# Half-width products for the dilated groups, and a head's values placed in front of the next head's scores

## The chip, the cores and the metric

The kernel runs on one core of one Trainium2 chip. The metric is the device time of one execution in microseconds (us); the time before is the median of three runs. TensorE (PE in the profile) multiplies matrices: the stationary operand is loaded by a weight load (PEld), then the other operand is streamed through it, and the result lands in PSUM. PSUM has eight banks here, each of 128 partitions by 512 words. VectorE (DVE), ScalarE (ACT) and GpSimd (POOL) work beside TensorE, and SyncE (SP) starts the loads of the weights from memory.

## What is computed

Two residual layers over 256 tokens of width 1024. The first mixes tokens with a gated short convolution, the second with dilated attention, and each has an MLP and a gated embedding behind it. The change is in the attention, which has eight heads of width 128. Each head is computed three times, in groups with three patterns of (window, dilation), and the three results are weighted by a softmax over their log-sums, which is the same as one softmax over all scores of the three groups together:

```python
DILATED_PATTERNS = ((128, 1), (512, 4), (2048, 16))
...
s = jnp.einsum('nbqhd,nbkhd->nbhqk', qb, kk) * (dh ** -0.5)
band = (rel >= 0) & (rel <= n_back)
...
o_g, lse_g = dilated_window_attention(q[:, :, g], k[:, :, g], v[:, :, g], window, dilation)
weights = jax.nn.softmax(jnp.stack(lses, axis=0), axis=0)
o = jnp.sum(weights[..., None] * jnp.stack(outs, axis=0), axis=0)
```

In group 1 a token attends only to tokens of its own residue modulo 4, in group 2 only to its own residue modulo 16.

## The kernel before

**Number formats.** Most products are made of operands split into a high and a low part (`hi`, `lo`, format fp32r): `lo*hi`, `hi*lo` and `hi*hi` are added up in one bank. Every loaded weight slab is split by ACT (L357, `whi`) and DVE (L296, `wlo`). The products of groups 1 and 2 in the attention are plain fp32 instead: L684 for the scores, L724 for the values.

**Layout.** From the second layer on, tokens are ordered by `residue_order` (L41): 64 tokens of one residue modulo 4 follow each other. There are two blocks `b` of 128 tokens, so that each block holds two whole residues, in its first and its second 64 rows. Group 1 and group 2 therefore need only the products of a block with itself, and of these only the two squares of 64 by 64 on the diagonal; the other two squares are computed too and are masked out.

**A head's steps.** `qk_out` rotates queries and keys (from the second head on, on POOL: L647 to L656), `qk_split` splits group 0. `v_out` (L662) scales the values out of the two banks `acc_v`: group 0 split into `v0`, groups 1 and 2 into `v12`. `scores` (L674) makes, for each block, three fp32r products of 256 columns for group 0 (L681) and one fp32 product of 128 by 128 for each of the groups 1 and 2 (L684), all in one bank of 512 columns; then mask and maximum (L687), exponential (L691) and division (L693) give the weights `sm`. `turn` (L695) transposes them: the half that belongs to groups 1 and 2 on DVE in squares of 32 (L701, L704), group 0 on TensorE (L708). `values` (L711) adds up the head's output in one bank: six fp32r products for group 0 (L718), then four fp32 products of 128 by 128 for groups 1 and 2 (L724); L735 and L736 split the result into `y`.

**The order.** `make_plan` (L139) writes down one list of blocks of weights (`w`, `n`, `t`: two or three products each, all issued at L393) and steps (`do`). TensorE follows it. In the loop over heads `h` (L199 to L206) the blocks of head `h` alternate with the steps of head `h-1`: `scores` stands behind the blocks of group 0, `turn` behind those of group 2, and `values` between the values' blocks 5 and 6. Head 1 is later by one place, and `values` of head 0 then stands in head 2. The last head's steps are laid between the blocks of the output projection `w_o`: three rounds of `w_o`, `scores`, two rounds, `turn`, one round, `values`, two rounds. A scheduler orders each engine's instructions by this program order, and puts in the waits.

**Buffers.** All banks come from one pool of eight (L262). Weights are split five slabs ahead of their use (`LOOK`, L34).

Of the kernel before, what the change touches and what calls it, by code (L numbers as in the profile page):

```python
# [9 lines left out]
F32 = mybir.dt.float32  # L10
# [5 lines left out]
P = 128  # L16
S = 256
# [237 lines left out]
def tile_trunk(ctx: ExitStack, tc: tile.TileContext, plan, slabs, ap, out):  # L255
# [11 lines left out]
    def act(name, dtype=F32):  # L267
        return apool.tile([P, 2, S], dtype, tag="act", name=name)
# [23 lines left out]
    def flat(t):  # L292
        return t.rearrange("p i s -> p (i s)")
# [285 lines left out]

    def masks_load():  # L580
        for b in (0, 1):
            mask[b] = apool.tile([P, 512], F32, tag="act", name=f"mask{b}")
            nc.sync.dma_start(mask[b], ap["mask"][:, b, :])

    def conv(c):
# [75 lines left out]

    def v_out(head):  # L662

        v0, v12 = act(f"v0_{head}", F32R), act(f"v12_{head}")
        for b in (0, 1):
            p, r = flat(close(("v", b, head))), rstd[3][:, b : b + 1]
            hi, lo = v0[:, b, :P], v0[:, b, P:]
            nc.scalar.activation(hi, p[:, :P], AF.Copy, scale=r)
            nc.vector.scalar_tensor_tensor(lo, p[:, :P], r, f32(hi), ALU.mult, ALU.subtract)
            nc.scalar.activation(v12[:, b, :], p[:, P : GROUPS * P], AF.Copy, scale=r)  # L670
        cur["v", head] = v0, v12


    def scores(head):  # L674
        weights = cur["pr", head] = pair(f"sm{head}", dtype=F32)[2]
        for b in (0, 1):
            own = slice(b * P, (b + 1) * P)
            ps = psum.tile([P, 512], F32, tag="ps", name=f"sc{head}_{b}")
            hi, lo, _ = state["qk"][head]
            for n, (q, k) in enumerate(((hi, hi), (hi, lo), (lo, hi))):  # L680
                nc.tensor.matmul(ps[:, :S], q[:, 0, own], k[:, 1, :], start=n == 0, stop=n == 2)  # L681
            for g in (1, 2):
                t = cur["qk", head, g]
                nc.tensor.matmul(ps[:, (g + 1) * P : (g + 2) * P], t[:, 0, own], t[:, 1, own], start=True, stop=True)  # L684
            sm = flat(weights[:, b])
            stats = [spool.tile([P, 1], F32, tag=f"st{n}_{b}", name=f"st{n}_{head}_{b}") for n in range(3)]
            nc.vector.tensor_tensor_reduce(  # L687
                out=sm, in0=ps, in1=mask[b], op0=ALU.add, op1=ALU.max, scale=SCALE, scalar=NEG, accum_out=stats[0]
            )
            nc.vector.tensor_scalar(stats[1], stats[0], -1.0, None, ALU.mult)  # L690
            nc.scalar.activation(sm, sm, AF.Exp, bias=stats[1], accum_out=stats[2])  # L691
            nc.vector.reciprocal(stats[2], stats[2])
            nc.scalar.activation(sm, sm, AF.Copy, scale=stats[2])  # L693

    def turn(head):  # L695

        sm = cur.pop(("pr", head))
        t = cur["pT12", head] = act(f"pT12_{head}")  # L700
        nc.vector.transpose(t, sm[:, :, 1, :])  # L701
        for q in range(4):
            rows, cols = (slice(n * 32, (n + 1) * 32) for n in (q, q ^ 1))
            nc.vector.transpose(t[cols, :, rows], sm[rows, :, 1, cols])  # L704
        ps = bank(f"tp{head}")
        for b in (0, 1):
            for n in (0, 1):
                nc.tensor.transpose(ps[:, n, b * P : (b + 1) * P], sm[:, b, 0, n * P : (n + 1) * P], ident)  # L708
        split_into("pT", head, ps)

    def values(head):  # L711
# [7 lines left out]
                    ps[:, 0, :], a, b[:, kb, :], start=kb == 0 and n == 0, stop=False, skip_group_check=True  # L719
                )  # L720
        t = cur.pop(("pT12", head))
        for b in (0, 1):
            for g in (0, 1):
                nc.tensor.matmul(  # L724
                    ps[:, 0, b * P : (b + 1) * P],
                    v12[:, b, g * P : (g + 1) * P],
                    t[:, b, g * P : (g + 1) * P],
                    start=False,
                    stop=g == 1,
                    skip_group_check=True,  # L730
                )
        if head % 2 == 0:
# [120 lines left out]
def masks():  # L853

    import numpy as np

    t = np.argsort([residue_order(t) for t in range(S)])
    m = np.full((P, 2, 512), NEG, np.float32)
    for b in range(2):
        q = t[b * P : (b + 1) * P, None]  # L860
        for keys, to, window, step in (
            (t, slice(0, S), 128, 1),
            (t[b * P : (b + 1) * P], slice(S, S + P), 512, 4),
            (t[b * P : (b + 1) * P], slice(S + P, S + 2 * P), 2048, 16),
        ):
            d = q - keys[None]
            m[:, b, to][(d >= 0) & (d <= window) & (d % step == 0)] = 0.0
    return m


# [56 lines left out]
```

## Time and profile before

| quantity | value |
|---|---|
| median of three runs | 777.29 us (777.19 to 777.32) |
| the profiled execution, its own time | 777.36 us |
| its span in the profile | 775.5 us |
| attention with its output projection | about 306 to 560 us of the span |
| one head in the steady state, from `scores` to `scores` | 28.63 us (395.49 to 424.12) |

How to read it: the span is what the hardware profiler saw, and 1.9 us of the device time lie around it. A row of a group of instructions gives the source line, the engine, the operation, output and inputs by name, shapes and the count; then busy time and the mean duration of one; then idle time of that engine ahead of them and what ended it. A row of a timeline gives the start in us, the length from the first start to the last end, and the same names; neighbours on one engine are merged with their count. TensorE's products are pipelined: one lasts longer than the distance to the next one's start, so costs on TensorE are read from distances of starts and not from durations. An fp32 product is two instructions on TensorE, each with a weight load of its own, so L684 and L724 have 64 instructions each for 32 products.

### The profile page before, as it was taken

How to read it: one execution, taken by the hardware profiler on the slowest of the kernel's cores; microseconds unless marked ns; L12 is line 12 of the kernel's file. 1: busy time of each engine (PE TensorE's matmuls, PEld its weight loads, DVE VectorE, ACT ScalarE, POOL GpSimd, SP SyncE). 2: the span in 40 equal slices, each digit the busy share in tenths (PEclk: the TensorE clock that was granted, in tenths of full speed). 3: DMA queues.
4: the chain of work that ended last, by engine and by line, in shares of the span. 5: the costliest groups of instructions: out<-in, count | busy, mean ns of one | idle time of the engine just before them, and what ended most of it. 6: DMA issues, size and time to landing. Idle time of an engine off the chain costs nothing.

```text
span 775.5 us, 12403 instructions
## 1 busy us (share of the span) xinstructions
PE 766.9 (99%) x4780; PEld 696.3 (90%) x4780; DVE 595.5 (77%) x863; ACT 439.4 (57%) x677; POOL 167.1 (22%) x110
## 2 busy tenths in 40 slices
PE   9999999999999999999999999999999999999996
PEld 8998998888888899989999989989988888888885
DVE  6898779898566668789789889887798887555664
ACT  7655565565444446557655655655665555444454
POOL 0000000000000000078867867865000000000002
PEclk9999999999999999999999999999999999999999
DMA  8965655655565554654546445456465655555521
GB/s 313 301 192 187 187 184 180 195 187 191 190 188 190 191 190 138 210 182 157 170 150 183 158 152 188 150 161 208 135 211 181 190 188 188 188 188 191 190 93 54
DMA packets 42538, 140.95 MB, mean 182 GB/s; under 512 B 4848, under 2 KB 6128, under 8 KB 42480
## 3 DMA queue, kind: packets, MB, share of 16 engines
q1 hardware_dynamic: 41904, 139.52, 55.9%
q8 instruction: 37, 0.61, 0.3%
q10 hardware_dynamic: 576, 0.66, 0.3%
q14 instruction: 21, 0.17, 0.1%
HBM read 139.10 MB, written 1.05 MB: 181 GB/s over the span
## 4 chain that ended last, share of the span: by engine, by line
PE 97%; issue 1%; DMA 1%; DVE 0%; POOL 0%; SPq 0%; POOLq 0%; DVEq 0%; ACT 0%
PE acc_u L393 23%; PE acc_d L393 23%; PE acc_qk L393 17%; PE acc_v L393 9%; PE acc_o L393 6%; PE acc_g L393 5%; PE acc_B L393 3%; PE acc_C L393 3%; PE acc_X L393 3%; PE o L724 1%; PE sc L684 1%; PE acc_p L393 1%; PE o L718 1%; PE sc L681 1%; DMA pt<-in_pT 1%
## 5 line engine op out<-in xcount | busy, mean ns | idle before, releaser
L296 DVE TENSOR_TENSOR wlo<-raw,whi 128x1024 fp32r<-128x1024 f32 (+2 forms) x277 | 353.2, 1280 | 125.6 <-ACT whi L357 122.7
L357 ACT ACTIVATE whi<-raw 128x1024 fp32r<-128x1024 f32 (+2 forms) x277 | 278.2, 1007 | 214.3 <-PE acc_d L393 77.1
L393 PE MATMUL acc_d<-u,whi 128*128 128x512 f32 x512 | 160.8, 395 | 0.0
L393 PE MATMUL acc_u<-x,whi 128*128 128x512 f32 x512 | 160.8, 395 | 0.0
L393 PE MATMUL acc_qk<-x,whi 128*128 128x512 f32 (+1 forms) x432 | 134.5, 368 | 0.0
L393 PEld LDWEIGHTS acc_d<-u,wlo 128*128 128x128 f32 x512 | 96.2, 188 | 22.7
L393 PEld LDWEIGHTS acc_u<-x,wlo 128*128 128x128 f32 x512 | 96.2, 188 | 22.5
L463 POOL TENSOR_TENSOR n<-v,power 128x2 f32<-128x2 f32 (+1 forms) x6 | 3.9, 650 | 517.1 <-DVE v L488 512.6
L393 PE MATMUL acc_qk<-x,wlo 128*128 128x256 f32 x384 | 108.0, 281 | 0.0
L393 PE MATMUL acc_u<-x,wlo 128*128 128x256 f32 x512 | 101.2, 278 | 0.0
L393 PE MATMUL acc_d<-u,wlo 128*128 128x256 f32 x512 | 100.9, 278 | 0.0
L393 PEld LDWEIGHTS acc_qk<-x,whi 128*128 128x128 f32 x432 | 78.0, 189 | 13.6
L650 POOL TENSOR_TENSOR rot<-qk,sinr 16x512 f32<-16x512 f32 x44 | 78.5, 1785 | 3.0
L393 PEld LDWEIGHTS acc_d<-u,whi 128*128 128x128 f32 x512 | 78.0, 189 | 0.0
L393 PEld LDWEIGHTS acc_u<-x,whi 128*128 128x128 f32 x512 | 78.0, 189 | 0.0
L393 PEld LDWEIGHTS acc_qk<-x,wlo 128*128 128x128 f32 x384 | 72.6, 189 | 0.0
L393 PE MATMUL acc_v<-whi,x 128*128 128x384 f32 x256 | 69.0, 340 | 0.0
L647 POOL TENSOR_TENSOR qk<-qk,cosr 128x512 f32<-128x512 f32 x22 | 37.4, 1698 | 51.4 <-DVE qk L413 41.0
L393 PEld LDWEIGHTS acc_v<-whi,x 128*128 128x128 f32 x256 | 46.6, 188 | 0.0
L393 PE MATMUL acc_o<-y,whi 128*128 128x256 f32 x256 | 46.3, 283 | 0.0
L393 PE MATMUL acc_v<-wlo,x 128*128 128x384 f32 x128 | 42.9, 335 | 0.0
L656 POOL TENSOR_TENSOR qk<-qk,rot 48x512 f32<-48x512 f32 x22 | 42.3, 1924 | 1.7
(176 smaller groups left out, 1036.2 us busy)
## 6 DMA issues: line engine op xcount, KB each, us to landing
raw<-in_w SPq DMA_DIRECT2D x230, 512.0 KB, 4.0
raw<-in_w SPq DMA_DIRECT2D x32, 384.0 KB, 3.1
raw<-in_w SPq DMA_DIRECT2D x10, 256.0 KB, 5.0
h<-in_xT SPq DMA_DIRECT2D x4, 256.0 KB, 5.0
mask<-in_mask SPq DMA_DIRECT2D x2, 256.0 KB, 4.3
gain<-in_gain SPq DMA_DIRECT2D x2, 256.0 KB, 4.3
out<-htg SPq DMA_DIRECT2D x2, 256.0 KB, 2.1
raw<-in_w ACTq DMA_DIRECT2D x2, 128.0 KB, 3.6
```

The source lines that it names most:

```text
L296: nc.vector.tensor_tensor(out, a, f32(b), ALU.subtract)
L357: nc.scalar.activation(hi[:, :width], t[:, :width], AF.Copy)
L393: nc.tensor.matmul(to, a, b, start=n == 0 and name not in opened, stop=n == len(products) - 1 and left[name, half if kind == "n" else 0] == 0,
L463: nc.gpsimd.tensor_tensor(y, v, power[:, : v.shape[1]], ALU.pow)
L647: engine.tensor_tensor(t, p, both(cosr), ALU.mult)
L650: engine.tensor_tensor(r[dst : dst + 16], p[src : src + 16], sinr[src : src + 16].unsqueeze(1).to_broadcast([16, 2, S]), ALU.mult,)
L656: engine.tensor_tensor(t[:48], t[:48], r[:48], ALU.add)
L681: nc.tensor.matmul(ps[:, :S], q[:, 0, own], k[:, 1, :], start=n == 0, stop=n == 2)
L684: nc.tensor.matmul(ps[:, (g + 1) * P : (g + 2) * P], t[:, 0, own], t[:, 1, own], start=True, stop=True)
L718: nc.tensor.matmul(ps[:, 0, :], a, b[:, kb, :], start=kb == 0 and n == 0, stop=False, skip_group_check=True)
L724: nc.tensor.matmul(ps[:, 0, b * P : (b + 1) * P], v12[:, b, g * P : (g + 1) * P], t[:, b, g * P : (g + 1) * P], start=False, stop=g == 1, ...
```

## The change

The products of groups 1 and 2 shrink to the squares of 64 by 64 that are needed, and their operands are stored accordingly: in a block's 64 rows of one residue, the scores of group 1 stand at the residue's own place and those of group 2 at the other's, so that both groups together take 128 columns in place of 256. `v_out` stores the values of groups 1 and 2 stacked in the same way, in one piece for each block, residue and group. The values' products are cut into halves of 64 output rows, whose squares write to the first or the second 64 partitions of the bank; so do those of the scores. The step `values` of a head no longer has a place of its own in the plan (except for the last head): `scores` of the next head calls it first, and the half-width products of both follow each other.

```diff
     for h in range(1, HEADS):
-        late, steps = h == 1, [[("do", what, h - 1)] for what in ("scores", "turn", "values")]
-        plan += qk(h, 0, range(NK)) + ([("do", "values", 0)] if h == 2 else []) + sums(h, 0)
-        plan += [("do", "qk_split", 0)] if late else steps[0]
-        plan += qk(h, 1, range(NK)) + sums(h, 1) + qk(h, 2, range(NK)) + steps[late ^ 1] + sums(h, 2)
-        plan += v(h, range(3)) + [("do", "qk_split", h)] + v(h, range(3, 6)) + steps[2 - late]
+        late, scores, turn = h == 1, [("do", "scores", h - 1)], [("do", "turn", h - 1)]
+        plan += qk(h, 0, range(NK)) + sums(h, 0) + ([("do", "qk_split", 0)] if late else scores)
+        plan += qk(h, 1, range(NK)) + sums(h, 1) + qk(h, 2, range(NK)) + (scores if late else turn) + sums(h, 2)
+        plan += v(h, range(3)) + [("do", "qk_split", h)] + v(h, range(3, 6)) + (turn if late else [])
...
-    plan += [x for k in (0, 1, 2) for j in range(NP) for x in mix("w_o", j, (k,))]
+    plan += [x for k in (0, 1) for j in range(NP) for x in mix("w_o", j, (k,))]
     plan.append(("do", "scores", last))
-    plan += [x for k in (3, 4) for j in range(NP) for x in mix("w_o", j, (k,))]
+    plan += [x for k in (2, 3, 4) for j in range(NP) for x in mix("w_o", j, (k,))]
...
 def v_out(head):
-            nc.scalar.activation(v12[:, b, :], p[:, P : GROUPS * P], AF.Copy, scale=r)
+            for r in (0, 1):
+                own, other = (slice(n * 64, (n + 1) * 64) for n in (r, 1 - r))
+                for g, to in ((1, own), (2, other)):
+                    nc.scalar.activation(
+                        v12[to, b, r * P : (r + 1) * P], p[own, g * P : (g + 1) * P], AF.Copy, scale=scale[own]
+                    )
...
 def scores(head):
+        if head:
+            values(head - 1)
         weights = cur["pr", head] = pair(f"sm{head}", dtype=F32)[2]
+        ps = [psum.tile([P, 512], F32, tag="ps", name=f"sc{head}_{b}") for b in (0, 1)]
+        for b in (0, 1):
+            for g in (1, 2):
+                t = cur["qk", head, g]
+                for r in (0, 1):
+                    of, at = slice(b * P + r * 64, b * P + (r + 1) * 64), S + (g - 1 ^ r) * 64
+                    nc.tensor.matmul(
+                        ps[b][r * 64 : (r + 1) * 64, at : at + 64], t[:, 0, of], t[:, 1, of], start=True, stop=True
+                    )
         for b in (0, 1):
...
-            for g in (1, 2):
-                t = cur["qk", head, g]
-                nc.tensor.matmul(ps[:, (g + 1) * P : (g + 2) * P], t[:, 0, own], t[:, 1, own], start=True, stop=True)
-            sm = flat(weights[:, b])
+            sm, p = flat(weights[:, b])[:, : S + P], ps[b][:, : S + P]
...
 def turn(head):
-        nc.vector.transpose(t, sm[:, :, 1, :])
-        for q in range(4):
-            rows, cols = (slice(n * 32, (n + 1) * 32) for n in (q, q ^ 1))
+        nc.vector.transpose(t[:, :, :P], sm[:, :, 1, :P])
+        for q, k in ((0, 1), (1, 0), (0, 2), (1, 3), (2, 0), (3, 1), (2, 3), (3, 2)):
+            rows, cols = (slice(n * 32, (n + 1) * 32) for n in (q, k))
             nc.vector.transpose(t[cols, :, rows], sm[rows, :, 1, cols])
...
 def values(head):
-        for b in (0, 1):
-            for g in (0, 1):
+        for n in range(4):
+            q, b, r = slice(n * 64, (n + 1) * 64), n // 2, n % 2
+            for m in (0, 1):
+                to = slice(m * 64, (m + 1) * 64)
                 nc.tensor.matmul(
-                    ps[:, 0, b * P : (b + 1) * P],
-                    v12[:, b, g * P : (g + 1) * P],
-                    t[:, b, g * P : (g + 1) * P],
+                    ps[to, 0, q],
+                    v12[:, b, r * P + m * 64 : r * P + (m + 1) * 64],
+                    t[:, b, r * 64 : (r + 1) * 64],
```

The masks shrink from 512 to 384 columns, with group 1 and 2 at the stacked places. With them the mask step (L687), the exponential (L691) and the division (L693) work on 384 columns in place of 512.

More of the change, by code (lines that the diff above doesn't have):

```diff
@@ L581, in masks_load @@
         for b in (0, 1):
-            mask[b] = apool.tile([P, 512], F32, tag="act", name=f"mask{b}")
+            mask[b] = apool.tile([P, S + P], F32, tag="act", name=f"mask{b}")
             nc.sync.dma_start(mask[b], ap["mask"][:, b, :])
@@ L665, in v_out @@
         for b in (0, 1):
-            p, r = flat(close(("v", b, head))), rstd[3][:, b : b + 1]
+            p, scale = flat(close(("v", b, head))), rstd[3][:, b : b + 1]
             hi, lo = v0[:, b, :P], v0[:, b, P:]
-            nc.scalar.activation(hi, p[:, :P], AF.Copy, scale=r)
-            nc.vector.scalar_tensor_tensor(lo, p[:, :P], r, f32(hi), ALU.mult, ALU.subtract)
-            nc.scalar.activation(v12[:, b, :], p[:, P : GROUPS * P], AF.Copy, scale=r)
+            nc.scalar.activation(hi, p[:, :P], AF.Copy, scale=scale)
@@ L671, in v_out @@
+            nc.vector.scalar_tensor_tensor(lo, p[:, :P], scale, f32(hi), ALU.mult, ALU.subtract)
+            for r in (0, 1):
[4 more added lines that the diff above has]
+                    )
         cur["v", head] = v0, v12
     def scores(head):
+        if head:
+            values(head - 1)
@@ L676, in scores @@
         for b in (0, 1):
             own = slice(b * P, (b + 1) * P)
-            ps = psum.tile([P, 512], F32, tag="ps", name=f"sc{head}_{b}")
             hi, lo, _ = state["qk"][head]
             for n, (q, k) in enumerate(((hi, hi), (hi, lo), (lo, hi))):
-                nc.tensor.matmul(ps[:, :S], q[:, 0, own], k[:, 1, :], start=n == 0, stop=n == 2)
-            for g in (1, 2):
-                t = cur["qk", head, g]
-                nc.tensor.matmul(ps[:, (g + 1) * P : (g + 2) * P], t[:, 0, own], t[:, 1, own], start=True, stop=True)
@@ L685, in scores @@
-            sm = flat(weights[:, b])
+                nc.tensor.matmul(ps[b][:, :S], q[:, 0, own], k[:, 1, :], start=n == 0, stop=n == 2)
+            sm, p = flat(weights[:, b])[:, : S + P], ps[b][:, : S + P]
             stats = [spool.tile([P, 1], F32, tag=f"st{n}_{b}", name=f"st{n}_{head}_{b}") for n in range(3)]
             nc.vector.tensor_tensor_reduce(
-                out=sm, in0=ps, in1=mask[b], op0=ALU.add, op1=ALU.max, scale=SCALE, scalar=NEG, accum_out=stats[0]
+                out=sm, in0=p, in1=mask[b], op0=ALU.add, op1=ALU.max, scale=SCALE, scalar=NEG, accum_out=stats[0]
@@ L721, in values @@
         t = cur.pop(("pT12", head))
[L722 to L723 removed]
+        for n in range(4):
+            q, b, r = slice(n * 64, (n + 1) * 64), n // 2, n % 2
+            for m in (0, 1):
+                to = slice(m * 64, (m + 1) * 64)
                 nc.tensor.matmul(
[L725 to L727 removed]
+                    ps[to, 0, q],
+                    v12[:, b, r * P + m * 64 : r * P + (m + 1) * 64],
+                    t[:, b, r * 64 : (r + 1) * 64],
                     start=False,
[L729 removed]
+                    stop=n == 3,
                     skip_group_check=True,
@@ L857, in masks @@
     t = np.argsort([residue_order(t) for t in range(S)])
-    m = np.full((P, 2, 512), NEG, np.float32)
+    m = np.full((P, 2, S + P), NEG, np.float32)
     for b in range(2):
         q = t[b * P : (b + 1) * P, None]
[L861 to L867, printed above, removed]
+        for r, rows in enumerate((slice(0, 64), slice(64, P))):
+            own = t[b * P : (b + 1) * P][rows]
+            for keys, at, window, step in (
+                (t, 0, 128, 1),
+                (own, S + r * 64, 512, 4),
+                (own, S + (1 - r) * 64, 2048, 16),
+            ):
+                d = q[rows] - keys[None]
+                m[rows, b, at : at + len(keys)][(d >= 0) & (d <= window) & (d % step == 0)] = 0.0
     return m
```

## The prediction

> **What bounds the kernel now.** I read the page first: the engines' shares, the granted clock, the chain that ended last.
>
> ```profile
> span 775.5 us, 12403 instructions
> PE 766.9 (99%) x4780; PEld 696.3 (90%) x4780; DVE 595.5 (77%) x863; ACT 439.4 (57%) x677; POOL 167.1 (22%) x110
> PEclk9999999999999999999999999999999999999999
> PE 97%; issue 1%; DMA 1%; DVE 0%; POOL 0%; SPq 0%; POOLq 0%; DVEq 0%; ACT 0%
> ```
>
> TensorE is busy for 99% of the span at full granted clock, and the chain is TensorE for 97%. A busy TensorE may still wait inside, so next comes the view of waits, asked for TensorE alone:
>
> ```profile
> PE warm L523 <- DVE power L519: 1.0, 1, 1.0
> PE acc_p L393 <- ACT whi L357: 0.2, 1, 0.2
> ```
>
> Two waits, both in the first microseconds (L523 is the warm-up); from there TensorE waits for nobody. So only TensorE time counts for this change, as long as the others keep their lead. Are they ahead?
>
> ```profile
> L357 ACT ACTIVATE whi<-raw 128x1024 fp32r<-128x1024 f32 (+2 forms) x277 | 278.2, 1007 | 214.3 <-PE acc_d L393 77.1
> 388.60:417.25 28.65, 28.65 (x178) 26.60 (x177) 24.50 (x34) 17.02 (x29) 20.89 (x13) 1.00 0.53 166
> ```
>
> ACT's splitting of weights waits for TensorE to free buffers (214.3 us of idle time ahead of it), so the supply of weights runs ahead. The second row is a window of one head's length, with busy time of PE, PEld, DVE, ACT, POOL: 28.65 us of TensorE beside 24.50 of DVE and 17.02 of ACT.
>
> **What the products cost now.** One head's `values`, then one head's `scores`, on TensorE's timeline, and the groups of the fp32 products:
>
> ```profile
> 385.90 0.33 PE L393 MATMUL acc_v<-wlo,x 128*128 128x384 f32 x1
> 386.07 0.33 PE L393 MATMUL acc_v<-whi,x 128*128 128x384 f32 x1
> 386.25 0.87 PE L718 MATMUL o<-pT,v 128*128 128x256 f32 x6
> 386.96 1.05 PE L724 MATMUL o<-pT,v 128*128 128x128 f32 x8
> 387.77 0.42 PE L393 MATMUL acc_v<-whi,x 128*128 128x384 f32 x1
> 388.02 0.34 PE L393 MATMUL acc_v<-wlo,x 128*128 128x384 f32 x1
> ...
> 395.49 0.51 PE L681 MATMUL sc<-qk 128*128 128x256 f32 x3
> 395.83 0.61 PE L684 MATMUL sc<-qk 128*128 128x128 f32 x4
> 396.20 0.61 PE L681 MATMUL sc<-qk 128*128 128x256 f32 x3
> 396.64 0.60 PE L684 MATMUL sc<-qk 128*128 128x128 f32 x4
> 397.00 0.36 PE L393 MATMUL acc_qk<-x,wlo 128*128 128x256 f32 x1
> ...
> L684 PE MATMUL sc<-qk 128*128 128x128 f32 x64 | 9.7, 274 | 0.0
> L724 PE MATMUL o<-pT,v 128*128 128x128 f32 x64 | 8.4, 275 | 0.0
> ```
>
> Eight instructions of L724 last 1.05 us in all and one lasts 0.275, so they start (1.05 - 0.275)/7 = 0.111 us apart. L684 gives (0.61 - 0.274)/3 = 0.112. The two groups have 64 instructions each: 128 x 0.111 = **14.2 us** of the kernel. That is all that the change can touch on TensorE; the fp32r products of L681 and L718 keep number and size.
>
> What makes 0.111? The sums over tokens at L478 are fp32 with the same 128-column weights, but stream only 2 columns:
>
> ```profile
> 30.27 0.54 PEld L478 LDWEIGHTS ssq<-ones,tot 128*128 128x128 f32 x4
> 30.73 0.19 PEld L393 LDWEIGHTS acc_C<-x,wlo 128*128 128x128 f32 x1
> 30.75 0.36 PE L393 MATMUL acc_C<-x,wlo 128*128 128x256 f32 x1
> 30.84 0.19 PEld L393 LDWEIGHTS acc_C<-x,whi 128*128 128x128 f32 x1
> ```
>
> Their four weight loads start (0.54 - 0.19)/3 = 0.117 us apart, and the next two 0.11: as far as with 128 columns streamed. **The load of the stationary operand sets the pace of these products**, so streaming 64 columns instead of 128 saves nothing by itself; what counts is what a load of 64 columns costs, and whether the loads and products of the two halves of the array run beside each other.
>
> **The change, part by part.** *Number of instructions.* Scores go from 32 fp32 products to 8 heads x 2 blocks x 2 groups x 2 residues = 64, values from 32 to 8 x 4 x 2 = 64: 256 instructions in place of 128.
>
> *Price of one.* No row has a 64-column load. Upper bound: 0.111 us, if a load costs the same at any width. One after the other at a cost by columns: half, 0.056. Lower bound: the least distance at which the trace lets things follow on TensorE. The product at 30.75 opens 0.02 behind its load, and the one at 396.20 opens 0.03 behind the last fp32 one, which started at 395.83 + 0.61 - 0.27 = 396.17 although that needs 0.11 more; so about 0.031, where neither load nor stream holds it. Totals: 28.4, 14.3 and 7.9 us, which is +14.2, +0.1 and -6.3 against now. The diff alternates the halves at each product (`r` in the inner loop of `scores`, `m` in that of `values`), but a product is two instructions, and both use one half. Of each pair I expect the second to follow at 0.056, and the next product in the other half at 0.031: mean 0.0435, 256 x 0.0435 = 11.1, **-3.1 us**. I take this value because it is the middle between the two ends that a load by columns allows.
>
> Beside this, the Trainium skill, "TensorE: Matmul & The Clock Gate", section "LDWEIGHTS (loading the stationary operand)", puts the load at its number of columns over 1.2 in ns: 107 ns for 128, which the 0.111 of the rows agrees with, and 53 for 64, which no run here shows yet; by it alone the sum would be near the +0.1.
>
> *Changes of width.* TensorE goes from full width to half width and back. `scores` of heads 1 to 7 has the values of the head before in front, so there are seven joint places, plus `scores` of head 0 and `values` of head 7: 9 places, 18 changes. The trace has only changes of format (L718 to L724 and back), and those are free: 386.96 + 8 x 0.111 + 0.17 for the first `acc_v` product (386.07 - 385.90) gives 388.02, and there its neighbour starts. Lower bound 0. Upper bound: the array runs empty at each change, which shows what now lies beside the next product, 0.275 - 0.111 = 0.164 us, so 18 x 0.164 = 3.0 us. I take one half-width load in the open, 0.056: 18 x 0.056 = **+1.0 us**, nearer to the rows' zero than to the other end.
>
> *The moved step.* `values` gets later by a piece of v and by group 0's blocks; what it needs is ready earlier relative to it. It takes its TensorE time along. `scores` now opens with the fp32 products, which need POOL's last group. For heads 1 to 6 their distance to POOL stays, since the time of `values` drops out behind `qk_out` and comes back in front of `scores`; for head 7 one round of `w_o` (8 blocks x 3 products of 256 columns; L718 has six of them in 386.96 - 386.25, 0.118 each: 2.8 us) no longer lies in between.
>
> ```profile
> 389.80 2.16 POOL L656 TENSOR_TENSOR qk<-qk,rot 48x512 f32<-48x512 f32 x1
> 533.44 2.16 POOL L656 TENSOR_TENSOR qk<-qk,rot 48x512 f32<-48x512 f32 x1
> 541.76 0.52 PE L681 MATMUL sc<-qk 128*128 128x256 f32 x3
> 391.43 0.84 ACT L670 ACTIVATE v<-acc_v,n 128x256 f32<-128x256 f32 x2
> L668 ACT ACTIVATE v<-acc_v,n 128x128 fp32r<-128x128 f32 x16 | 5.9, 367 | 8.8 <-PE acc_v L393 8.8
> L670 ACT ACTIVATE v<-acc_v,n 128x256 f32<-128x256 f32 x16 | 6.7, 471 | 6.0 <-DVE v L669 6.0
> L687 DVE CUSTOM_DVE_ANT_0 sm<-sc,mask 128x512 f32<-128x512 f32 x16 | 10.9, 683 | 2.5 <-PE sc L684 2.5
> L691 ACT ACTIVATE sm<-sm,st 128x512 f32<-128x512 f32 x16 | 11.6, 722 | 13.5 <-DVE st L690 13.5
> L704 DVE STREAM_TRANSPOSE pT<-sm 32x64 f32<-32x64 f32 x32 | 7.6, 237 | 0.8
> ```
>
> Head 2's POOL work ends at 391.96, 3.5 us ahead of the scores at 395.49. Head 7's ends at 535.60, and the scores come at 541.76 - 2.8 = 539.0, still 3.4 us later. No wait. No DMA moves; the masks are two loads that only get smaller.
>
> *ACT and DVE.* `v_out` gets eight pieces of 128 columns per head for two of 256. At L668's 0.367 (same columns) that is 8 x 0.367 - 2 x 0.471 = +2.0 us of ACT per head. L691 and L693 lose up to a quarter of 0.72 in four instructions, -0.7. DVE: four more squares in `turn`, +0.95, less half of the big one (-0.35) and a quarter of 0.68 twice (-0.34): +0.3. Against 24.50 and 17.02 of 28.65 these stay hidden. The ACT pieces hold the `acc_v` banks longer: their last read ends at 391.43 + 0.84 = 392.3 now and 394.3 then, and with two banks each for `acc_v`, group 0 and the scores and one for the output, the eighth and the held ones aren't wanted before group 1's blocks at 397.00. Cover of 2.7 us; without it, each us of lateness would cost one per head.
>
> **Sum:** 777.36 (the profiled execution's own time: span 775.5 and 1.9 around it) - 3.1 + 1.0 = 775.3; it lies 0.07 above the median of the runs, so on the median's scale **775.2 us**.
>
> **The rivals.** A measurement of this kernel can tell about 0.2%, 1.6 us, from no change.
>
> *Forecast: the halves overlap and a change of width costs little.* From -6.3 (0.031 and free changes) to -1.6: 771.0 to 775.7. For it: 0.03 us is enough to follow where the array is free, and the order alternates halves. Against: the pairs in one half. Chance 0.48.
>
> *The two terms cancel.* Overlap at 0.0435 with a full drain, -3.1 + 3.0 = -0.1, or no overlap and free changes, +0.1: 777.2 to 777.4. Chance 0.25.
>
> *Slower: no overlap, and the array drains.* Loads go through one port one after the other (0.056 each, nothing gained), and each of the 18 changes exposes 0.164: +0.1 + 3.0 = 780.4; with a half-width load in the open at each as well, another 1.0: 781.4. It decides as soon as a change costs more than the saving over 18; with the overlap taken above that is 3.1/18 = 0.17 us, without it any drain. For it: the loads already stand back to back at 0.111 today, so the trace shows a single load pipe that is full; and 0.164 us of each product lies under its successor, cover that a drain takes away. Against: the trace's changes of format don't drain. Chance 0.19.
>
> The Trainium skill bears on this in "TensorEngine Tiling (Array Packing)", section "Key Properties": a change of the tiling mode drains TensorE, while separate tiles load and multiply in parallel. With the rows' prices that would be the second rival's -0.1; no run here shows either half of it so far, and the drain speaks against the change.
>
> *The change doesn't make a product cheaper.* If a half-width load costs what a full one does, twice the instructions are +14.2: 791.5 us. For it: the rows at L478 show that fewer streamed columns don't help. Against: nothing in them varies the loaded columns. Chance 0.06. *A wait appears* (banks held by `v_out`, scores before POOL), 0.6 us in each of seven heads: 4.2 - 2.1 = +2.1, 779.4. Chance 0.02.
>
> **How the numbers follow.** Faster by over 0.2%: 0.48; within: 0.25; slower: 0.19 + 0.06 + 0.02 = 0.27. The range reaches from the lower bound of the forecast to the upper end of the slower rival, 771.0 to 781.4; only the unhalved load and larger waits lie outside.
>
> **What would show it.** In the profile after, L724's and L684's successors have 128 instructions each. Their distance of starts settles the price: about 0.03 and 0.056 in turn, 0.056 throughout, or 0.111. The distance from the last fp32r product to the first half-width one, and back, less the usual 0.118, is the price of a change. TensorE's waits should stay at the two of the start; a wait for ACT `v` or POOL `qk` would prove the cover wrong. L670 should show 128 columns at about 0.37 us, 128 times. The forecast is wrong if a change of width costs over 0.1 us or the halves take turns.

## The result: slower, by a wait that the prediction did not see

The changed kernel takes 781.27 us (781.07 to 781.64, 4 runs) against 777.24 us (4 runs) of the kernel before: ratio 1.0053, 95% interval 1.0036 to 1.0071. The forecast was 2 us faster; the kernel is 4.0 us slower. Line numbers change with the edit: L681 is now L698, L684 is L691, L718 is L731, L724 is L739, L670 is L673, L708 is L721, L687 is L701, L393 is L392, L357 is L356, L296 is L295, L412/L413 are L411/L412, L430 is L429, L647 to L656 are L646 to L655. The kernels of the experiments have numbers of their own, a few lines further on.

The page after, first the lines that answer to those shown of before:

```profile
span 779.3 us, 12752 instructions
PE 766.5 (98%) x4908; PEld 692.0 (89%) x4908; DVE 601.3 (77%) x895; ACT 449.9 (58%) x725; POOL 171.2 (22%) x110
PE 80%; DVE 6%; issue 5%; POOL 4%; ACT 4%; DMA 1%; SPq 0%; POOLq 0%; DVEq 0%; ACTq 0%
```

TensorE's busy time fell by 0.4 us while the span grew by 3.8, and the chain that ended last is no longer TensorE alone: it now runs through DVE, POOL and ACT too. TensorE's waits name the place (in a row of waits: us in total, times, the longest), and windows around it show what the wait costs beyond itself (columns: window, its length, busy time of PE, PEld, DVE, ACT, POOL, then the granted TensorE clock):

```profile
PE tp L721 <- ACT sm L707: 3.8, 1, 3.8
...
PE o L731 <- DVE pT L295: 0.3, 1, 0.3
...
356.30:360.30 4.00, 0.20 (x3) 0.01 (x1) 4.00 (x5) 0.70 (x3) 3.86 (x3) 0.94 0.32 96
360.30:364.00 3.70, 3.70 (x15) 3.48 (x16) 3.59 (x7) 2.89 (x5) 2.48 (x2) 0.61 0.34 107
```

Head 0's transposes (`tp`) wait nearly 4 us, once, for the softmax weights `sm`. In that time DVE and POOL are busy almost without a break (4.00 and 3.86 of 4.00), and ACT is busy for 0.70 only. Behind the wait the granted clock is 0.61, and the products of `acc_v` start 0.32 us apart and not 0.17 until about 363: some 1.4 us more, 0.39 of 3.7. TensorE also waits at the half-width scores of five later heads, for POOL, 0.1 to 0.3 us each and 1.3 in all (the row at 456.28 below lasts 0.95 us, the one at 399.42, where nothing waits, 0.64), and 0.5 us at the last head's `values`.

The half-width products themselves are cheaper than the forecast took them. One joint place on TensorE, the scores of a later head that wait for POOL, all half-width scores, and the pieces on ACT:

```profile
398.11 0.87 PE L731 MATMUL o<-pT,v 128*128 128x256 f32 x6
398.90 0.69 PE L739 MATMUL o<-pT,v 128*64 128x64 f32 x16
399.42 0.64 PE L691 MATMUL sc<-qk 128*64 128x64 f32 x16
399.99 0.74 PE L698 MATMUL sc<-qk 128*128 128x256 f32 x4
...
456.28 0.95 PE L691 MATMUL sc<-qk 128*64 128x64 f32 x16
...
L691 PE MATMUL sc<-qk 128*64 128x64 f32 x128 | 6.1, 227 | 0.3
L673 ACT ACTIVATE v<-acc_v,n 64x128 f32<-64x128 f32 x64 | 23.2, 362 | 19.4 <-DVE v L669 18.6
```

Sixteen instructions of L691 last 0.64 us and one 0.227: they start (0.64 - 0.227)/15 = 0.028 us apart. The last row is the culprit, as the experiments will show: the eight pieces per head in which ACT takes the values out of PSUM, 0.362 each. Head 0's, and what DVE and POOL do behind them, in the kernel before and then in the changed one:

```profile
338.25 0.84 ACT L670 ACTIVATE v<-acc_v,n 128x256 f32<-128x256 f32 x2 [1.80 <-DVE v L669]
340.40 0.74 DVE L413 TENSOR_TENSOR qk<-acc_qk,qk 128x256 f32<-128x256 f32 x2
341.06 0.67 DVE L296 TENSOR_TENSOR qk<-qk,qk 128x512 fp32r<-128x512 f32 x1
341.21 3.42 POOL L647 TENSOR_TENSOR qk<-qk,cosr 128x512 f32<-128x512 f32 x1 [5.37 <-DVE qk L413]
```

```profile
337.52 3.00 ACT L673 ACTIVATE v<-acc_v,n 64x128 f32<-64x128 f32 x8 [1.80 <-DVE v L669]
340.96 0.76 DVE L412 TENSOR_TENSOR qk<-acc_qk,qk 128x256 f32<-128x256 f32 x2 [1.22 <-ACT qk L411]
341.89 1.75 DVE L295 TENSOR_TENSOR qk<-qk,qk 128x512 fp32r<-128x512 f32 x1 [0.18 <-ACT qk L429]
341.80 1.30 POOL L646 TENSOR_TENSOR qk<-qk,cosr 128x512 f32<-128x512 f32 x1 [6.68 <-DVE qk L412]
```

DVE's sums for head 1 now wait 1.22 us for ACT, and POOL starts 0.09 us ahead of DVE's split of head 0's `qk`, where it started 0.15 behind.

### The profile page after: what moved, and what is told of

It is laid out like the page before. It is cut to its first block, busy times and chain, and to the rows that moved or that the text cites. A ratio compares the mean times of both kernels' runs of the same rounds, so it can differ in the third digit from the quotient of the medians.

```text
span 779.3 us, 12752 instructions
## 1 busy us (share of the span) xinstructions
PE 766.5 (98%) x4908; PEld 692.0 (89%) x4908; DVE 601.3 (77%) x895; ACT 449.9 (58%) x725; POOL 171.2 (22%) x110
## 4 chain that ended last, share of the span: by engine, by line
PE 80%; DVE 6%; issue 5%; POOL 4%; ACT 4%; DMA 1%; SPq 0%; POOLq 0%; DVEq 0%; ACTq 0%
PE acc_u L392 23%; PE acc_d L392 23%; PE acc_qk L392 9%; PE acc_g L392 5%; PE acc_v L392 4%; PE acc_o L392 4%; PE acc_B L392 3%; PE acc_C L392 3%; PE acc_X L392 3%; DVE wlo L295 3%; POOL rot L649 2%; ACT v L673 1%; ACT whi L356 1%; POOL qk L646 1%; PE acc_p L392 1%
## 5 line engine op out<-in xcount | busy, mean ns | idle before, releaser
L295 DVE TENSOR_TENSOR wlo<-raw,whi 128x1024 fp32r<-128x1024 f32 (+2 forms) x277 | 356.0, 1293 | 130.3 <-ACT whi L356 127.7
L356 ACT ACTIVATE whi<-raw 128x1024 fp32r<-128x1024 f32 (+2 forms) x277 | 277.7, 1006 | 207.6 <-PE acc_d L392 77.1
L392 PE MATMUL acc_u<-x,whi 128*128 128x512 f32 x512 | 160.9, 395 | 0.0
L392 PE MATMUL acc_d<-u,whi 128*128 128x512 f32 x512 | 160.8, 395 | 0.0
L392 PE MATMUL acc_qk<-x,whi 128*128 128x512 f32 (+1 forms) x432 | 135.7, 371 | 0.0
L392 PEld LDWEIGHTS acc_d<-u,wlo 128*128 128x128 f32 x512 | 96.2, 188 | 22.7
L392 PEld LDWEIGHTS acc_u<-x,wlo 128*128 128x128 f32 x512 | 96.2, 188 | 22.6
L392 PE MATMUL acc_qk<-x,wlo 128*128 128x256 f32 x384 | 107.5, 280 | 0.0
L392 PE MATMUL acc_u<-x,wlo 128*128 128x256 f32 x512 | 101.2, 278 | 0.0
L392 PE MATMUL acc_d<-u,wlo 128*128 128x256 f32 x512 | 100.9, 278 | 0.0
L392 PEld LDWEIGHTS acc_qk<-x,whi 128*128 128x128 f32 x432 | 78.1, 189 | 14.7
L649 POOL TENSOR_TENSOR rot<-qk,sinr 16x512 f32<-16x512 f32 x44 | 81.2, 1846 | 3.0
L392 PEld LDWEIGHTS acc_d<-u,whi 128*128 128x128 f32 x512 | 78.0, 189 | 0.0
L392 PEld LDWEIGHTS acc_u<-x,whi 128*128 128x128 f32 x512 | 77.9, 189 | 0.0
L392 PEld LDWEIGHTS acc_qk<-x,wlo 128*128 128x128 f32 x384 | 72.5, 189 | 0.0
L392 PE MATMUL acc_v<-whi,x 128*128 128x384 f32 x256 | 68.1, 340 | 0.0
L646 POOL TENSOR_TENSOR qk<-qk,cosr 128x512 f32<-128x512 f32 x22 | 38.9, 1769 | 54.9 <-DVE qk L412 47.3
L392 PEld LDWEIGHTS acc_v<-whi,x 128*128 128x128 f32 x256 | 47.1, 191 | 0.0
L392 PE MATMUL acc_o<-y,whi 128*128 128x256 f32 x256 | 46.2, 283 | 0.0
L392 PE MATMUL acc_v<-wlo,x 128*128 128x384 f32 x128 | 43.2, 337 | 0.0
L655 POOL TENSOR_TENSOR qk<-qk,rot 48x512 f32<-48x512 f32 x22 | 42.5, 1934 | 1.7
```

The source lines that it names most:

```text
L295: nc.vector.tensor_tensor(out, a, f32(b), ALU.subtract)
L356: nc.scalar.activation(hi[:, :width], t[:, :width], AF.Copy)
L392: nc.tensor.matmul(to, a, b, start=n == 0 and name not in opened, stop=n == len(products) - 1 and left[name, half if kind == "n" else 0] == 0,
L646: engine.tensor_tensor(t, p, both(cosr), ALU.mult)
L649: engine.tensor_tensor(r[dst : dst + 16], p[src : src + 16], sinr[src : src + 16].unsqueeze(1).to_broadcast([16, 2, S]), ALU.mult,)
L655: engine.tensor_tensor(t[:48], t[:48], r[:48], ALU.add)
```

## The experiments

**First question: which part makes the wait?** Three parts could: the eight pieces (theory P), the moved step, or the stacked layout (both theory M). Four kernels answer this; the kernel before, measured beside them, has 776.8 us.

*The pieces alone*, put into the kernel before:

```diff
-            nc.scalar.activation(v12[:, b, :], p[:, P : GROUPS * P], AF.Copy, scale=r)
+            for rows in (slice(0, 64), slice(64, P)):
+                for g in (0, 1):
+                    nc.scalar.activation(
+                        v12[rows, b, g * P : (g + 1) * P], p[rows, (g + 1) * P : (g + 2) * P], AF.Copy, scale=r[rows]
+                    )
```

> The kernel before, with nothing changed but that the values of groups 1 and 2 are copied out of PSUM in eight pieces of 64 by 128 per head, as in the changed kernel, instead of two of 128 by 256 (same result). Theory P (the pieces): ACT is held 2.1 us longer behind head 0's values, head 1's sums for group 0 and with them DVE and POOL come later, and head 0's transposes on TensorE wait for the softmax: a wait of 2 to 5 us at tp, and 780 to 783 us. Theory M (the moved step and the stacked layout cause the wait): no wait at tp, 777.0 to 777.8 us. The products are those of before, so nothing is gained on TensorE.

Measured: 782.32 us, ratio 1.0073 (1.0061 to 1.0086). Its waits:

```profile
PE tp L712 <- ACT sm L697: 3.6, 2, 3.4
```

The same wait at the same place, in a kernel with the old products, the old layout and the old order. Theory P stands, and M isn't needed. (Head 0's eight pieces take 2.51 us here; in the changed kernel, which also moves half of them to other rows, 3.00.)

*The pieces taken out of the changed kernel:*

```diff
-            for r in (0, 1):
...
+            nc.scalar.activation(v12[:, b, :], p[:, P : GROUPS * P], AF.Copy, scale=scale)
```

> The changed kernel with the two copies of 128 by 256 of the kernel before in place of the eight pieces; the values of groups 1 and 2 are then not stacked by residue, so the attention's values are not those of the reference, and only the copies' number and shape differ. Theory P: the wait at tp goes, also most of the waits of the scores for POOL, and the half-width products are left with their gain of 0.3 us a head: 774 to 775.5 us. Theory M: the wait at tp stays, 780 to 782 us.

Measured: 774.23 us, 0.9966 (0.9952 to 0.9979), and TensorE's only wait is that of the warm-up. That is the gain of the half-width products without the cost of feeding them.

*The order alone*: the kernel before with the changed `make_plan`, and `values(head - 1)` at the head of `scores`.

> The kernel before with the changed order alone: values called at the head of the next scores, and the changed places in w_o; products, masks and copies are those of before. Theory P: no wait at tp, 777.0 to 777.8 us. Theory M: a wait at tp of some us and 779 to 782 us.

Measured: 777.05 us, 1.0002 (0.9993 to 1.0011), no wait at `tp`. With full-width products the place of `values` is worth nothing.

*The changed kernel in the old order*: the plan of before, without the call in `scores`.

> The changed kernel with the order of the kernel before: values at their own place, so TensorE changes its width 32 times and not 18. Theory P: the wait at tp stays (the pieces are there), and the seven more visits add their entry and exit, about 0.3 us each by the trace of the changed kernel (0.16 on the way in, 0.15 on the way out): 782.5 to 784 us. If a change of width costs next to nothing, 781 to 781.7 us.

Measured: 784.76 us, 1.0103 (1.009 to 1.0117), a little beyond the expected 784, since the last head's `values` also waits 1.6 us for `pT`, where the changed kernel waits 0.5. TensorE visits half width 15 times here and not 16, so 30 changes and not the 32 of the expectation: head 0's `values` stands right in front of head 1's `scores` in the old order too. The price of a change of width can be read from the distance of two heads' `scores`, here against the kernel with the pieces first that follows below; neither waits there (the old order first):

```profile
372.99 0.86 PE L697 MATMUL sc<-qk 128*128 128x256 f32 x5
401.68 0.98 PE L697 MATMUL sc<-qk 128*128 128x256 f32 x6
```

```profile
394.26 0.23 PE L691 MATMUL sc<-qk 128*64 128x64 f32 x2
422.59 0.23 PE L691 MATMUL sc<-qk 128*64 128x64 f32 x2
```

28.69 against 28.33 us a head: one more visit to half width costs 0.36 us, 0.18 for each change. So placing `values` in front of the next `scores` does pay, for six heads, with half-width products only: at their own places these would give 28.69 against the 28.63 of before, that is nothing. The six visits (2.2 us) and the longer wait at the end (1.1) are 3.3 of the 3.5 us that this kernel takes beyond the changed one.

**Second question: is it the number of the pieces or their place?** In the changed kernel the pieces stand behind DVE's low part of the values, and DVE is late with that in head 0. Pieces first, for head 0 alone and for all heads (same result):

```diff
             nc.scalar.activation(hi, p[:, :P], AF.Copy, scale=scale)
-            nc.vector.scalar_tensor_tensor(lo, p[:, :P], scale, f32(hi), ALU.mult, ALU.subtract)
             for r in (0, 1):
...
+            nc.vector.scalar_tensor_tensor(lo, p[:, :P], scale, f32(hi), ALU.mult, ALU.subtract)
```

> The changed kernel, with head 0's eight pieces alone issued ahead of DVE's low part of the values (v0, lo) instead of behind it; same result. In the changed kernel the pieces sit behind DVE's rotation of head 0's queries and keys, until 337.5 us of the span, although ACT had been free before. Theory P: head 1's sums come at their old time, the wait at tp (4.0 us) and the TensorE clock lost behind it (1.4 us) go, the waits of the scores for POOL in the later heads (about 1.1 us) stay: 775.5 to 776.5 us. Rival: the eight pieces cost by their number wherever they stand, and the wait stays at over 2 us: 779 us or more.

Measured, head 0 alone: 778.3 us, 1.0024 (1.0015 to 1.0033), 1.8 us above the upper end. The wait at `tp` is gone, but another takes its place, at the scores of head 2:

```profile
PE sc L694 <- POOL qk L655: 2.0, 1, 2.0
...
PE o L734 <- DVE pT L295: 0.3, 1, 0.3
```

So the stall isn't special to head 0. The expectation took it for that, and took the later heads' waits for POOL as they were in the changed kernel, where the stop at `tp` had come before them. With the other heads' pieces moved as well, this wait goes too:

> The same for all heads: pieces ahead of DVE's low part; same result. Theory P: the waits of the scores for POOL shrink too, since ACT is free again when the next head's sums come: 774.2 to 775.2 us. Rival: the waits for POOL come from elsewhere (DVE's eight squares in turn, ahead of the sums) and stay, 775.5 to 776.5 us.

Measured, all heads: 773.99 us, 0.9966 (0.9954 to 0.9978), faster than both kernels, with the same 64 pieces of the same length:

```profile
PE warm L522 <- DVE power L518: 1.0, 1, 1.0
PE acc_p L392 <- ACT whi L356: 0.2, 1, 0.2
...
332.04 1.47 ACT L672 ACTIVATE v<-acc_v,n 64x128 f32<-64x128 f32 x4
333.54 0.37 ACT L668 ACTIVATE v<-acc_v,n 128x128 fp32r<-128x128 f32 x1
333.81 1.47 ACT L672 ACTIVATE v<-acc_v,n 64x128 f32<-64x128 f32 x4
...
337.50 0.39 ACT L411 ACTIVATE qk<-acc_qk 128x256 f32<-128x256 f32 x1 [0.40 <-PE acc_qk L392]
```

The pieces run at 332 to 335, where ACT had time, and at 337.5 ACT waits for head 1's sums instead of keeping them waiting. All waits in the attention, those for POOL as well, are gone. So it is the pieces' place and not their number.

**Third question: how does a hold of about 2 us on ACT become 4 us on TensorE?** Two theories: a full queue hands lateness on in step; or DVE and POOL block each other, and the hold turns round which goes first (lock). Three runs with copies added behind head 0's values failed as a test:

> The kernel before with ACT held behind head 0's two copies of the values by two more copies of 64 by 128 (they write again what stands there; same result), 0.31 us each by the pieces run: 0.6 us at this one place, nothing else. Theory lock: the hold does nothing until head 1's queries and keys are added up later than POOL can start on them; DVE's split of the head's group 0 (0.67 us when it starts 0.15 us ahead of POOL) then starts behind POOL and waits for it (1.75 us), and the 768-column splits behind it do the same (1.81 to 4.0 us). At 0.6 us it is near that point: a wait at tp of either under 0.3 us or over 2 us, nothing between. Theory queue: each us of hold gives about as much wait at tp, less the slack of about 1.5 us: no wait here.

> The same with four more copies, 1.2 us of hold. Theory lock: beyond the point where POOL starts first, the full wait of 2 to 4 us at tp, as with eight pieces in all heads, and 779 to 782 us. Theory queue: no wait or under 0.5 us, 776.5 to 777.5 us.

> The same with seven more copies, 2.2 us of hold, a little more than the eight pieces (1.7 us more than two copies). Theory lock: the same wait as with four copies to 0.7 us, since it is POOL's instructions that are waited for and not ACT's; 779 to 783 us. Theory queue: a wait at tp 1 us longer than with four copies.

Measured: 777.0, 776.86 and 776.72 us, ratios 1.0001 (0.9992 to 1.0011), 1.0 (0.9991 to 1.001) and 0.9999 (0.9989 to 1.0008); no wait at `tp`. The scheduler had laid the added copies between head 1's sums, so DVE's sums and its split of head 0's `qk` were not held back; the split still started 0.14 to 0.15 us ahead of POOL, and the two theories were not set apart. But with four and with seven copies DVE lost its turn one place later, while it waited 0.30 us for ACT. The seven:

```profile
341.56 3.64 DVE L296 TENSOR_TENSOR wlo<-raw,whi 128x768 fp32r<-128x768 f32 x2 [0.30 <-ACT whi L357]
349.75 0.69 DVE L690 CUSTOM_DVE_ANT_0 sm<-sc,mask 128x512 f32<-128x512 f32 x1 [0.34 <-PE sc L687]
```

The two splits last 3.64 us (1.81 where DVE keeps its turn, below), and yet the softmax's maximum (L690) still waits 0.34 us for TensorE and not the other way round. So a lost turn costs TensorE nothing while DVE has slack.

To hold the sums, the copies themselves were cut finer instead, at head 0 of the kernel before alone: four, six and eight pieces in place of two, which stay together.

> The kernel before, but head 0's values of groups 1 and 2 are copied in four pieces of 128 by 128 in place of two of 128 by 256 (other heads as before, same result): ACT is held about 0.3 us longer there, and the scheduler puts no other copy between them. Theory lock: head 1's sums are still done before POOL could get ahead of DVE's split, or at the very edge: no wait at tp, or the full one. Theory queue: no wait at tp. 776.5 to 777.5 us.

> The same with six pieces, four of them of 64 by 128: about 1 us longer than before. Theory lock: DVE's split of group 0 starts behind POOL and lasts 1.75 us in place of 0.67, and the splits behind it too: a wait at tp of 2 us or more, 779 us or more. Theory queue: a wait of 3.5 less about 0.75 us, 2.8 us or less, in step with the hold.

> The same with the eight pieces of the changed kernel, at head 0 alone: 1.7 us longer than before. Both theories: a wait at tp of 3.4 to 4 us, as with eight pieces in all heads, and 781 to 783 us. Theory lock: the difference to six pieces is small or none, since the lateness comes from POOL's instructions; theory queue: 0.7 us more wait than with six.

| copies at head 0 | ACT holds, us | DVE's split of head 0's `qk` starts | POOL starts | wait at `tp`, us | time, us (ratio) |
|---|---|---|---|---|---|
| 2 (before) | 0.84 | 341.06 | 341.21 | none | 776.9 |
| 4 | 1.14 | 340.66 | 340.82 | none | 776.85 (0.9998, 0.9989 to 1.0008) |
| 6 | 1.75 | 340.96 | 340.87 | 2.6 | 780.26 (1.0049, 1.0034 to 1.0064) |
| 8 | 2.50 | 341.49 | 341.39 | 3.4 | 782.15 (1.0069, 1.0054 to 1.0084) |

The traces do not start at the same moment, so starts compare within a row of the table. The waits, with six pieces and with eight:

```profile
PE tp L714 <- ACT sm L699: 2.8, 2, 2.6
...
PE tp L714 <- ACT sm L699: 3.4, 1, 3.4
```

Four pieces, DVE and POOL:

```profile
340.00 0.74 DVE L413 TENSOR_TENSOR qk<-acc_qk,qk 128x256 f32<-128x256 f32 x2
340.66 0.67 DVE L296 TENSOR_TENSOR qk<-qk,qk 128x512 fp32r<-128x512 f32 x1
341.26 1.81 DVE L296 TENSOR_TENSOR wlo<-raw,whi 128x768 fp32r<-128x768 f32 x2
...
349.85 0.69 DVE L693 CUSTOM_DVE_ANT_0 sm<-sc,mask 128x512 f32<-128x512 f32 x1 [1.20 <-PE sc L690]
...
340.82 3.42 POOL L647 TENSOR_TENSOR qk<-qk,cosr 128x512 f32<-128x512 f32 x1 [5.36 <-DVE qk L413]
```

Six pieces:

```profile
340.03 0.76 DVE L413 TENSOR_TENSOR qk<-acc_qk,qk 128x256 f32<-128x256 f32 x2
340.96 1.76 DVE L296 TENSOR_TENSOR qk<-qk,qk 128x512 fp32r<-128x512 f32 x1 [0.17 <-ACT qk L430]
342.65 3.99 DVE L296 TENSOR_TENSOR wlo<-raw,whi 128x768 fp32r<-128x768 f32 x2
...
352.03 0.68 DVE L693 CUSTOM_DVE_ANT_0 sm<-sc,mask 128x512 f32<-128x512 f32 x1
...
340.87 1.30 POOL L647 TENSOR_TENSOR qk<-qk,cosr 128x512 f32<-128x512 f32 x1 [5.43 <-DVE qk L413]
```

The sums (L413) start at the same time, within 0.03 us. But the split behind them needs ACT's high part (L430), which with six pieces comes 0.17 us late, and POOL is off 0.09 us ahead of DVE. With DVE ahead, DVE's split lasts 0.67 us and POOL's product 3.42; with POOL ahead, POOL's lasts 1.30 and DVE's 1.76, and the next two 768-column splits last 3.99 together and not 1.81. In these rows whoever starts first runs at full speed, and the other waits for it. That gives DVE 1.1 + 2.2 us of lateness from a hold of 0.6, more in the next pair (4.88 us there), and the softmax's maximum (L693) comes at 352.03 and not at 349.85. The times with four and with six pieces alone would fit either expectation; what decides is the step and these rows. From six to eight pieces the wait grows by 0.8 for 0.75 of hold, as the queue theory has it: once POOL is ahead, lateness is handed on in step, and the lock theory's "small or none" for that was wrong. At that rate 0.6 us less hold than with six pieces would leave a wait of 2.0, and with four pieces there is none: nothing at +0.3 us, 2.6 us at +0.9. So the step is the lock, once it takes more than DVE's slack.

The Trainium skill has this in "SBUF — State Buffer", section "SBUF: two separate sides": a DVE operation with two SBUF inputs and a GpSimd operation that reads SBUF use one pair of ports under an exclusive lock, the first to start keeps it for the whole instruction, and the other blocks fully. The rows with 0.67 against 1.76 us on DVE and 3.42 against 1.30 on POOL agree with it.

**Fourth question: what do the half-width products cost, and can the joint place be better?** Halves not in turn: loops reordered so that four products of one half follow each other, on top of the kernel with the pieces first.

> The one with the pieces first for all heads, but with the half-width products ordered so that four (values) or four (scores) products of one half follow each other, instead of halves in turn; same result. If the two halves of the array overlap only where neighbours are in different halves, an instruction costs 0.056 us in place of 0.029: 32 x 0.027 = 0.87 us a head, 7 us in all, 781 to 783 us. If the price of 0.029 comes from loads of half the width alone, it stays at 774.2 to 775.2 us.

Measured: 777.28 us, 1.0006 (0.9998 to 1.0015), no wait at `tp`: 3.3 us slower than with the halves in turn, and between the two expectations, so that neither holds. TensorE's timeline:

```profile
423.04 0.79 PE L739 MATMUL o<-pT,v 128*64 128x64 f32 x13
423.61 0.27 PE L691 MATMUL sc<-qk 128*64 128x64 f32 x1
423.66 0.22 PE L739 MATMUL o<-pT,v 128*64 128x64 f32 x1
423.72 0.22 PE L691 MATMUL sc<-qk 128*64 128x64 f32 x1
...
424.51 0.50 PE L698 MATMUL sc<-qk 128*128 128x256 f32 x2
```

The 32 instructions take 424.51 - 423.04 = 1.47 us where the alternating order took 399.99 - 398.90 = 1.09. Scores even start ahead of values that are in front of them in the program, and each of the two groups goes on at 0.06 us (423.66, 423.72, 423.78 and 423.72, 423.78). It looks as if each half had a queue of its own; how far one may run ahead of the other was not measured. So the overlap doesn't need strict alternation, but alternation saves 0.38 us a head.

*Full-width products first*, then all half-width ones of values and scores, on top of the pieces first:

```diff
-        if head:
-            values(head - 1)
+        finish = values(head - 1, True) if head else None
...
+        if finish:
+            finish()
         for b in (0, 1):
             for g in (1, 2):
```

> The previous one, with the order inside the joint place changed: the full-width products of values and scores first, then all 32 half-width instructions of both; same result. The half-width scores then come 1.5 us later against POOL, and the way back to full width goes straight to the blocks of weights. If the 512-column products behind the joint place are slowed (236 in place of 230 ns) by the way back into full-width split products, that goes or stays with the new neighbour: it is worth 0.2 us a head. Expected 773 to 775 us; if only waits mattered and none are left, as the previous one.

Measured: 773.63 us, 0.9961 (0.9949 to 0.9974), the fastest of the study, 3 us faster than the kernel before; 0.4 us less than the one with the pieces first.

## Why the prediction was wrong, point by point

- **"So only TensorE time counts for this change, as long as the others keep their lead"**: the condition was right and its check was not. The lead was checked for the weights and for POOL, by busy shares and by ends in the kernel before, not for what stands behind the edited instructions in ACT's own queue.
- **"*ACT and DVE*: +2.0 us of ACT per head ... Against 24.50 and 17.02 of 28.65 these stay hidden"** is the step that failed. The size was right: eight pieces take 3.00 us in the changed kernel against 0.84, +2.2. That they stay hidden was concluded from busy shares, and the cover named, the `acc_v` banks until 397.00, was not the one that mattered. Behind the pieces on ACT stand head 1's sums and the high part of head 0's `qk`; DVE's split waits for that, POOL gets in front by 0.09 us, and TensorE waits 4.0 us at `tp`. Taking the pieces out (774.23 us) or moving them (773.99) removes the whole loss.
- **"No wait"** for POOL at the scores (3.5 us of cover) failed by the same cause: POOL's ends were taken as fixed, while the pieces made the sums late that POOL starts from (1.3 us over five heads).
- **Price of a half-width instruction**, 0.0435 taken: measured 0.029, just under the lower bound of 0.031 (the joint place above has 32 in 1.09 us, the way out included; inside it is 0.028). The reason given was wrong as well: the two instructions of a product do not take turns with the next product; each half goes on at 0.058 us, and the two halves run beside each other. The term is 256 x 0.029 = 7.4 and not 11.1, so -6.8 and not -3.1 us.
- **Changes of width**, 0.056 taken: measured 0.36 for a visit, 0.18 a change, at the upper bound of 0.164 for an array that runs empty. 18 x 0.18 = +3.2 and not +1.0. By the prediction's own sign (over 0.1 us a change) this step failed too. In the joint place above about 0.08 us of a visit lies on the way in (398.70 to 398.90, 0.118 as usual) and 0.12 on the way out (399.84 to 399.99, less 0.028); the first full-width products behind are slower too. The Trainium skill's "TensorEngine Tiling (Array Packing)", section "Key Properties", has it that separate tiles work in parallel, and that a change of mode drains. The pairs 0.007 us apart (below) and the 0.18 a change agree with it, though no trace shows the draining itself.
- The two wrong sizes nearly cancel: -6.8 + 3.2 = -3.6, and 6 x 0.19 = +1.1 of slower neighbours (below) leave -2.5, where -2.1 was forecast. The kernel without waits has 0.9966 of the time before, -2.7 us. So without the wait the forecast's time would have come out by luck: that the halves overlap was right, that a change of width costs little was not.
- **The slower rival** (no overlap, and a drain: 780.4 to 781.4) has the measured time by luck: the price of a change is about its own, but the halves overlap, and what makes the kernel slow is the wait. That 781.27 lies inside the stated range rests on this rival alone. *A wait appears* was the right rival, with the banks and POOL as its place, 4.2 us where the waits and the clock behind them took 7.2, and a chance of 0.02.
- **DVE: +0.3 us a head, hidden**: the named terms came out (+7.5 us for the squares, -2.1 for the big transpose, -2.7 for the maximum: +2.7 in all). Busy time rose by more, 595.5 to 601.3, mostly in the splits, which last longer where POOL is in front. DVE's amount of work never showed as a bound, its order did.
- **"128 times"**, the count of L670's pieces, was a slip: eight in each of eight heads are 64, as the row of L673 has it. The sum went by eight a head.

The sum for the changed kernel's profile: 4.0 (wait at `tp`) + 1.4 (clock) + 1.3 (POOL, five heads) + 0.5 (last values) - 8 x 0.30 (28.63 less 28.33) = +4.8 us in the attention; the span has +3.8, and the stretch ahead of the attention was 0.7 us shorter in that execution, so +4.5 is to be explained.

## What to carry to other kernels

Where an edit makes an engine busier, don't compare its busy share with the bound: read what stands behind the new instructions in its queue, and who is waiting for that. On engines that block each other, being late by a tenth of a microsecond can cost microseconds, because it decides who goes first; it costs nothing while the loser has slack. When a cheap helper (here copies out of PSUM) is needed in more pieces, issue it where its engine is idle, ahead of any instruction whose partner is late.

## What the runs showed that was not expected

TensorE's two halves behave like two queues: in the alternating order, instructions start in pairs 0.007 us apart, one pair every 0.058; in the grouped order scores overtook values. The 512-column products behind a joint place are slower: a pair of `wlo` and `whi` products takes 0.36 us (402.33 to 402.69) where it took 0.35 before (398.60 to 398.95); the mean distance from the `whi` product to the next is 0.236 for 0.230, which over 32 pairs is about 0.19 us, in each of six heads. It lasts until the next plain fp32 products (`tp`).

```profile
402.33 0.40 PE L392 MATMUL acc_qk<-x,whi 128*128 128x512 f32 x1
402.57 0.28 PE L392 MATMUL acc_qk<-x,wlo 128*128 128x256 f32 x1
402.69 0.40 PE L392 MATMUL acc_qk<-x,whi 128*128 128x512 f32 x1
```

It stayed in all but one of the six heads with the full-width products first, so its cause is open. And the wait of 4 us cost more than itself: the granted clock is 0.61 in the 3.7 us behind it.
